# Byte positions of the weight tiles, LN1 in pairs with two evicting engines, and earlier FFN sums in a one-core decoder layer

## Chip, cores and metric

One Trainium2 chip, one core. The metric is the device time of one execution in microseconds (us). The kernel before takes 1160.0 us, the median of 3 runs (1159.33 to 1160.42).

## What is computed

One layer of a hybrid decoder on 512 tokens of width 1024, in float32:

```python
proj = x @ w_in
q, k, v, f_logit, z, xbc, dt_raw, gate_logit = split(proj)
attn_d = forgetting_attention(q, k, v, log_f) @ w_proj_attn
ssm_d = mamba2_branch(z, xbc, dt_raw, ...) @ w_proj_ssm
mixed = (gates[0] * attn_d + gates[1] * ssm_d) @ w_out
x = layer_norm(alpha * x + mixed, ln1_g, ln1_b)                  # LN1
h = (silu(x @ w_ffn_gate) * (x @ w_ffn_up)) @ w_ffn_down         # FFN, hidden width 2816
x = layer_norm(alpha * x + h, ln2_g, ln2_b)
```

## The kernel before

All large products run on TensorE in float32r with both operands split in a high and a low part (`split`, L81: ScalarE copies the high part, VectorE subtracts it). `mm3` (L115) then issues three matmuls, high x high, low x high and high x low, into one PSUM bank. Weights come through four `raw` tiles, three `whi` and three `wlo` tiles, all of 4 KB per partition (`stile`, L71).

The order of the work is the program's order on each engine, as a scheduler lays it out; the tile pools make an engine wait where a buffer is still in use. The stages are: the input projection with the attention and the Mamba-2 heads, group by group; the branch gates and `w_proj_attn`; `w_out` by two pairs of token tiles (`wo_half`, L843); LN1; the FFN; the down projection (`gemm_down`, L153, with `evac_res`, L687); the second layer norm with the output.

**LN1.** `wo_half` leaves the sums of a token tile in `xr[tt]` with the statistics of its two halves. `moments` (L692) makes mean and variance (VectorE) and the power -1/2 (POOL), and `normalise` (L846) scales the 1024 columns, one token tile after the other. `x1_transposed` (L850) turns eight 128x128 blocks on TensorE into two PSUM banks and evicts each block with an ACTIVATE (scale and bias per partition) into `xf`.

**FFN.** The gate and up products use seven half-size products in place of eight (Strassen-like), named P1 to P7, on blocks of 512 hidden columns (the sixth has 256): classes `Gemm` (L732) and `ffn_block` (L822). There are 12 Gemms, G0, U0, G1, U1 and so on (gate, up). Each uses the weight quarters a11, a12, a22 and two sums of quarters, s1 and s3. A sum is loaded by two DMAs (`load`, L750): SP's queue copies the first quarter, then POOL's queue adds the second one to it in place. `op` (L762) makes the high and low part (`wh`, `wl`) of one product's weights; for P6 and P3 VectorE first adds two loaded tiles (L766, L768). `multiply` (L788) has 24 matmuls of 256 streamed columns (12 in the last block), so the 12 Gemms have 10 x 7 x 24 + 2 x 7 x 12 = 1848. The weights are the stationary operand here; the streamed ones are `b11`, `b21`, `nt1`, `nt2`, `t3`, `b22`, `t4`, made of `xf`. The products run in this order: `rest` (L933) lists them, `op` runs two products ahead, and loads are issued here:

```python
        if p_ == "P7" and i + 3 < len(rest):
            rest[i + 3][0].load("a11", "a12", "s1")
        if p_ == "P4" and i + 1 < len(rest):
            rest[i + 1][0].load("s3", "a22")
```

The eight tiles `rq0` to `rq7` hold the loaded quarters in a ring (L756); G0 and U0 have places written out by hand (L862).

**Down projection.** The hidden tiles (`T` for block 0, then `ht...`) are stationary and the weights `whi`, `wlo` are streamed, 512 columns each: 22 x 4 x 2 x 3 = 528 matmuls.

**Byte positions.** A tile's position in a partition follows from the sizes of the tiles allocated before it. All the large tiles are multiples of 512 bytes, so what differs between stages is a position modulo 512. Call the *distance* of a matmul the start of the stationary operand less that of the streamed one, modulo 512. Before: up to `w_out` every distance of such products is 0. In the FFN `b11`, `b21` lie at 448 and the other streamed tiles at 320; the weight tiles of the pool `wop0` lie at 448 and those of `wop1` at 320. Pairs of products alternate between the pools, so half of the FFN's matmuls have distance 0 and half 128 or 384. In the down projection `whi`, `wlo` lie at 448 and the hidden tiles at 320: distance 384.

Of the kernel before, what the change touches and what calls it, by code (L numbers as in the profile page):

```python
# [17 lines left out]
P = 128  # L18
# [19 lines left out]
def tile_hybrid_decoder_layer(  # L38
# [8 lines left out]
    nc = tc.nc  # L47
    x, out = x[0], out[0]
# [17 lines left out]
    sba = pool(right1, "sba", "right")  # L66
    rawp = pool(right1, "rawp", "right")
    wst = pool(right1, "wst", "right")
    stream = {"raw": (rawp, 4), "whi": (wst, 3), "wlo": (wst, 3)}

    def stile(tag, dtype):  # L71
        p_, n = stream[tag]
        return p_.tile([P, 1024], dtype, name=tag, bufs=n)

    ident = cst0.tile([P, P], F32, name="ident")
    make_identity(nc, ident)
    neghalf = cst0.tile([P, 4], F32, name="neghalf")
# [10 lines left out]
    def cps():  # L88
        return psum.tile([P, T], F32, name="cps", bufs=4)
# [1 line left out]

    BUFS = {"v": 2, "th": 2, "bT": 2, "cT": 2, "btok": 2, "cbm": 2, "xst": 2, "xdt": 2, "hn": 2, "ab": 6, "y": 4,
            "dx": 1, "yo": 1, "xw": 1, "sq": 1, "xtok": 2, "gz": 1, "nw": 1, "uh": 1, "ul": 1, "sd": 4}
    HOME = {t: sba for t in ("hn", "ab", "y", "dx", "yo", "xw", "sq", "nw")}
    HOME["sd"] = sdp

    def slot(tag, shape=(P, T), dtype=F32):
# [346 lines left out]
    for p_ in ("uh", "ul"):  # L444
        t = big(p_, 2)
# [243 lines left out]
        nc.vector.scalar_tensor_tensor(out=o, in0=o, scalar=ALPHA, in1=ps, op0=ALU.mult, op1=ALU.add)  # L689
        nc.vector.bn_stats(out=st6[tt][:, half, :], in_=o)  # L690

    def moments(tt):  # L692
        mv = cst0.tile([P, 4], F32, name="mv", bufs=2)
        nc.vector.bn_aggr(out=mv[:, 0:2], in_=st6[tt])
        nc.vector.tensor_scalar(out=mv[:, 2:3], in0=mv[:, 1:2], scalar1=EPS, scalar2=None, op0=ALU.add)
        nc.gpsimd.tensor_tensor(out=mv[:, 2:3], in0=mv[:, 2:3], in1=neghalf[:, 0:1], op=ALU.pow)
        return mv

    def layer_norm(tt, gb, parts=1):
        mv = moments(tt)  # L700
# [31 lines left out]
    class Gemm:  # L732
# [17 lines left out]
        def load(self, *names):  # L750
            src = {"a11": ((1, 1),), "a12": ((1, 2),), "s1": ((2, 1), (2, 2)), "s3": ((2, 1), (1, 1)), "a22": ((2, 2),)}
            for nm in names:
                if self.slots:
                    i = self.slots[nm]
                else:
                    i, rq_order[0] = rq_order[0], (rq_order[0] + 1) % 8  # L756
                t = self.raw[nm] = rqp.tile([P, 1024], F32, name="rq", tag=f"rq{i}", bufs=1)[:, 0:4 * self.F]
                nc.sync.dma_start(out=self.v(t), in_=self.q(*src[nm][0]))
                for s_ in src[nm][1:]:
                    nc.gpsimd.dma_start(out=self.v(t), in_=self.q(*s_), accum_op=ALU.add)  # L760

        def op(self, p_):  # L762

            r = self.raw
            if p_ == "P6":
                nc.vector.tensor_tensor(out=r["a11"], in0=r["s1"], in1=r["a11"], op=ALU.add)  # L766
            elif p_ == "P3":
                nc.vector.tensor_tensor(out=r["a12"], in0=r["a11"], in1=r["a12"], op=ALU.add)  # L768
            t = r[{"P1": "a11", "P2": "a12", "P6": "a11", "P5": "s1", "P7": "s3", "P3": "a12", "P4": "a22"}[p_]]
            wp = wops[nops[0] // 2 % 2]  # L770
            nops[0] += 1
            o = [wp.tile([P, 1024], F32R, name="w" + i, bufs=2)[:, 0:4 * self.F] for i in "hl"]
            split(*o, t)
            self.ops[p_] = [self.v(i) for i in o]

# [70 lines left out]
    def normalise(tt):  # L846
        mv = moments(tt)
        nc.vector.tensor_scalar(out=xr[tt], in0=xr[tt], scalar1=mv[:, 0:1], scalar2=mv[:, 2:3], op0=ALU.subtract, op1=ALU.mult)

    def x1_transposed(tt):  # L850
        for i in range(2):
            ps = cps()
            for k in range(4):
                kt = 4 * i + k
                nc.tensor.transpose(out=ps[:, k * P:(k + 1) * P], in_=xr[tt][:, kt * P:(kt + 1) * P], identity=ident)
            for k in range(4):
                kt = 4 * i + k
# [29 lines left out]
    hb.tile([P, 8], F32, name="pad2")  # L887
    tp = pool(ctx, "tp", "left")
    top = pool(left2, "top", "left")
    wops.append(pool(left2, "wop1", "left"))  # L890
    tmp2 = pool(left2, "tmp2", "left")

    def t_tile(dtype=F32):
# [42 lines left out]
            rest += [(g_, p_) for p_ in ("P1", "P2", "P6", "P5", "P7", "P3", "P4")]  # L936
    AHEAD = 2
    for i, (g_, p_) in enumerate(rest):
        if p_ == "P7" and i + 3 < len(rest):
            rest[i + 3][0].load("a11", "a12", "s1")  # L940
        if p_ == "P4" and i + 1 < len(rest):
            rest[i + 1][0].load("s3", "a22")
        if i == 0:
            for k in range(1, AHEAD):
                rest[k][0].op(rest[k][1])
        if i + AHEAD < len(rest):
            rest[i + AHEAD][0].op(rest[i + AHEAD][1])
        g_.run(p_)
# [74 lines left out]
```

## Time and profile before

| | us |
|---|---|
| median of 3 runs | 1160.0 |
| the profiled execution | 1159.04 |
| its span (first to last instruction) | 1157.3 |
| TensorE matmuls busy | 1125.0 (97%) |
| TensorE weight loads busy | 946.7 (82%) |
| VectorE busy | 772.4 (67%) |
| ScalarE busy | 532.2 (46%) |
| GpSimd (POOL) busy | 135.3 (12%) |
| DMA | 134.2 MB, mean 116 GB/s |

The busy shares are of the whole span. Matmuls overlap each other in the pipeline, so a busy share of 97% doesn't say how fast they follow each other; for that the start of one is taken from the start of the next.

### The profile page before, as it was taken

What the parts mean: (1) busy time and instruction counts of PE and PEld (TensorE: products, weight loads), DVE (VectorE), ACT (ScalarE), POOL (GpSimd) and SP (SyncE); (2) the same over time, 40 slices, a digit from 0 to 9 for tenths busy, and PEclk for the clock granted to TensorE, in tenths of its full rate; (3) what the DMA queues carried; (4) which work ended last, traced back from release to release, by engine and by line L of the source; (5) the groups of instructions that cost most, each with busy time, mean ns of one, the idle gap of its engine ahead of it and who ended that gap; (6) DMA issues with size and microseconds to landing.
All of it is one profiled execution on the core that took longest, in us unless ns stands there. A gap on an engine that the chain in (4) does not pass through costs nothing.

```text
span 1157.3 us, 15804 instructions
## 1 busy us (share of the span) xinstructions
PE 1125.0 (97%) x6086; PEld 946.7 (82%) x6086; DVE 772.4 (67%) x1213; ACT 532.2 (46%) x928; POOL 135.3 (12%) x167
## 2 busy tenths in 40 slices
PE   7999999999999999999999999999999999999997
PEld 5887777778777788777777888888999999988885
DVE  3679964883886664888697434547787777667326
ACT  3376763453542432665566443207554454452210
POOL 3003130030231100211110000021101111100001
PEclk9999999999999999999999999999999999999999
DMA  8344243233231233221321255283767786465211
GB/s 247 91 131 127 74 126 93 73 119 100 84 100 55 91 91 91 57 59 53 92 56 56 80 158 163 85 224 88 189 145 195 175 196 155 93 230 176 92 55 73
DMA packets 115771, 134.20 MB, mean 116 GB/s; under 512 B 5636, under 2 KB 93936, under 8 KB 115568
## 3 DMA queue, kind: packets, MB, share of 16 engines
q1 hardware_dynamic: 99328, 112.80, 31.8%
q0 software_dynamic: 14640, 14.10, 7.6%
q10 hardware_dynamic: 1728, 6.29, 1.6%
q8 instruction: 48, 0.79, 0.3%
q14 instruction: 27, 0.22, 0.1%
HBM read 128.78 MB, written 4.26 MB: 115 GB/s over the span
## 4 chain that ended last, share of the span: by engine, by line
PE 49%; DVE 2%; ACT 1%; DMA 1%; issue 0%; DVEq 0%; ACTq 0%
PE gps L116 11%; PE gps L117 11%; PE gps L118 11%; PE cps L117 5%; PE cps L116 5%; PE cps L118 5%; PE cps L429 1%; PE cps L435 1%; DMA rq<-in_w_ffn_gate_dram 1%; ACT xf L858 0%; DVE xr L705 0%; PE cps L407 0%; PE cps L408 0%; DVE xr L704 0%; DVE st L690 0%
## 5 line engine op out<-in xcount | busy, mean ns | idle before, releaser
L83 DVE TENSOR_TENSOR wlo<-raw,whi 128x1024 fp32r<-128x1024 f32 x127 | 156.1, 1230 | 209.7 <-ACT whi L82 209.2
L82 ACT CAST whi<-raw 128x1024 fp32r<-128x1024 f32 x127 | 133.2, 1049 | 271.0 <-PE gps L118 109.9
L116 PE MATMUL gps<-xh,whi 128*128 128x512 f32 x456 | 181.3, 398 | 0.0
L117 PE MATMUL gps<-xl,whi 128*128 128x512 f32 x456 | 181.1, 397 | 0.0
L118 PE MATMUL gps<-xh,wlo 128*128 128x512 f32 x456 | 180.9, 397 | 0.0
L82 ACT CAST wh<-rq 128x1024 fp32r<-128x1024 f32 (+1 forms) x84 | 82.1, 981 | 105.8 <-PE cps L117 43.9
L83 DVE TENSOR_TENSOR wl<-rq,wh 128x1024 fp32r<-128x1024 f32 (+1 forms) x84 | 95.0, 1132 | 38.3 <-ACT wh L82 38.2
L116 PEld LDWEIGHTS gps<-xh,whi 128*128 128x128 f32 x456 | 85.9, 188 | 16.4 <-issue 0.2
L117 PEld LDWEIGHTS gps<-xl,whi 128*128 128x128 f32 x456 | 86.0, 189 | 16.2 <-issue 0.2
L118 PEld LDWEIGHTS gps<-xh,wlo 128*128 128x128 f32 x456 | 86.0, 188 | 15.5
L116 PE MATMUL gps<-whi,xh 128*128 128x512 f32 x192 | 75.9, 396 | 3.4 <-ACT xh L82 3.4
L118 PE MATMUL gps<-whi,xl 128*128 128x512 f32 x192 | 76.1, 396 | 0.0
L117 PE MATMUL gps<-wlo,xh 128*128 128x512 f32 x192 | 75.8, 395 | 0.0
L214 DVE SCALAR_TENSOR_TENSOR t_v<-gps,cw,t_v 128x511 f32<-128x511 f32 (+2 forms) x72 | 53.5, 745 | 3.9 <-ACT t_v L211 3.1
L118 PE MATMUL gps<-t_uh,wlo 128*128 128x512 f32 x128 | 51.0, 399 | 0.0
L117 PE MATMUL gps<-t_ul,whi 128*128 128x512 f32 x128 | 51.0, 398 | 0.0
L116 PE MATMUL gps<-t_uh,whi 128*128 128x512 f32 x128 | 50.5, 394 | 0.0
L116 PEld LDWEIGHTS gps<-whi,xh 128*128 128x128 f32 x192 | 36.6, 191 | 12.1 <-ACT xh L82 4.1
L760 POOL DMA_DIRECT2D rq<-in_w_ffn_gate_dram x12 | 15.5, 1294 | 256.8 <-DMA t_sd<-in_x_dram 164.0
L414 ACT ACTIVATE t_y<-t_y,sm 128x128 f32<-128x128 f32 (+1 forms) x64 | 35.7, 559 | 19.3 <-DVE sm L412 17.7
L296 ACT ACTIVATE t_ab<-t_ab,acum 128x128 f32<-128x128 f32 x128 | 41.4, 390 | 5.8 <-DMA t_ab<-ac_d 3.9
L117 PEld LDWEIGHTS gps<-wlo,xh 128*128 128x128 f32 x192 | 36.5, 190 | 8.0 <-DVE wlo L83 0.5
(565 smaller groups left out, 2780.6 us busy)
## 6 DMA issues: line engine op xcount, KB each, us to landing
raw<-in_w_in_dram SPq DMA_DIRECT2D x80, 512.0 KB, 3.7
rq<-in_w_ffn_gate_dram SPq DMA_DIRECT2D x25, 512.0 KB, 4.9
rq<-in_w_ffn_up_dram SPq DMA_DIRECT2D x25, 512.0 KB, 4.8
raw<-in_w_ffn_down_dram SPq DMA_DIRECT2D x22, 512.0 KB, 3.8
t_ab<-ac_d SPq DMA_DIRECT2D x32, 256.0 KB, 3.3
raw<-in_w_proj_ssm_dram SPq DMA_DIRECT2D x16, 512.0 KB, 3.4
rq<-in_w_ffn_gate_dram POOLq DMA_DIRECT2D x10, 512.0 KB, 7.8
rq<-in_w_ffn_up_dram POOLq DMA_DIRECT2D x10, 512.0 KB, 6.2
```

Source lines behind the costliest of these rows:

```text
L82: nc.scalar.copy(out=hi, in_=src)
L83: nc.vector.tensor_tensor(out=lo, in0=src, in1=hi.bitcast(F32), op=ALU.subtract)
L116: nc.tensor.matmul(out=o, lhsT=l[0], rhs=r[0], start=start, stop=False, skip_group_check=skip)
L117: nc.tensor.matmul(out=o, lhsT=l[0], rhs=r[1], start=False, stop=False, skip_group_check=skip)
L118: nc.tensor.matmul(out=o, lhsT=l[1], rhs=r[0], start=False, stop=stop, skip_group_check=skip)
L214: nc.vector.scalar_tensor_tensor(out=v[:, sh:], in0=ps[:, 0:T - sh], scalar=cw[:, k, blk:blk + 1], in1=v[:, sh:], op0=ALU.mult, op1=ALU.add)
L296: nc.scalar.activation(out=m[:, r, :], in_=m[:, r, :], func=AF.Relu, scale=-1.0, bias=acum[:, c, h:h + 1])
L414: nc.scalar.activation(out=pt[:, 0:n], in_=pt[:, 0:n], func=AF.Exp, scale=-1.0, bias=sm[:, 2:3], accum_out=sm[:, 0:1])
L429: nc.tensor.transpose(out=ps[:, o:o + P], in_=pr[i][:, kb * P:(kb + 1) * P], identity=ident)
L435: nc.tensor.matmul(out=po[:, kb * P:], lhsT=vt[:, kb, hh, :], rhs=pT[kb][j], start=kb == 0 and j == 0, stop=kb == NT - 1 and j == 1)
L760: nc.gpsimd.dma_start(out=self.v(t), in_=self.q(*s_), accum_op=ALU.add)
```

## The change

It has four parts.

- *Positions.* Small unused tiles (`offset`) are allocated between the tiles of the FFN and of the down projection. Every streamed FFN tile is then at 288 modulo 512, and the four pairs `wh`, `wl` at 480, 448, 0 and 384: distances 192, 160, 224 and 96. In the down projection the hidden tiles are at 288 and the three pairs `whi`, `wlo` at 288, 96 and 128: distances 0, 192 and 160. The tile `gz` moves to another pool of the same stage; distances up to `w_out` stay 0.
- *LN1 in pairs.* `moments` and `normalise` take two token tiles: one addition and one power for both.
- *Two engines evict.* In `x1_transposed` the first PSUM bank is evicted by four ACTIVATEs as before, the second by two TENSOR_TENSORs of VectorE over 4x128 columns (multiply, then add).
- *Loads.* a11, a12 and s1 of the next Gemm are loaded at P1 (for G1 at U0's P7, as before), s3 and a22 at P7 in place of P4. The ring is walked in the order 0, 1, 3, 4, 5, 6, 2, 7.

```diff
+HB_OFF, B_OFF, W_OFF, D_OFF = 512, 160, (0, 480, 224, 384, 352), (0, 320, 32, 320)
     def stile(tag, dtype):
-        p_, n = stream[tag]
-        return p_.tile([P, 1024], dtype, name=tag, bufs=n)
+        p_, n, *off = stream[tag]
+        if not off:
+            return p_.tile([P, 1024], dtype, name=tag, bufs=n)
+        i = at_.get(tag, 0)
+        at_[tag] = i + 1
+        if i < n and off[0]:
+            offset(p_, off[0][i], f"d{i}")
+        t = p_.tile([P, 1024], dtype, name=tag, tag=f"{tag}{i % n}", bufs=1)
...
+    def offset(p_, n, nm):
+        if n:
+            p_.tile([P, n // 4], F32, name="off" + nm)
-    HOME = {t: sba for t in ("hn", "ab", "y", "dx", "yo", "xw", "sq", "nw")}
+    HOME = {t: sba for t in ("hn", "ab", "y", "dx", "yo", "xw", "sq", "nw", "gz")}
-    def moments(tt):
-        mv = cst0.tile([P, 4], F32, name="mv", bufs=2)
-        nc.vector.bn_aggr(out=mv[:, 0:2], in_=st6[tt])
-        nc.vector.tensor_scalar(out=mv[:, 2:3], in0=mv[:, 1:2], scalar1=EPS, scalar2=None, op0=ALU.add)
-        nc.gpsimd.tensor_tensor(out=mv[:, 2:3], in0=mv[:, 2:3], in1=neghalf[:, 0:1], op=ALU.pow)
+    def moments(tts):
+        mv = cst0.tile([P, 2, 4], F32, name="mv", bufs=2)[:, 0:len(tts), :]
+        for i, tt in enumerate(tts):
+            nc.vector.bn_aggr(out=mv[:, i, 0:2], in_=st6[tt])
+        nc.vector.tensor_scalar(out=mv[:, :, 2], in0=mv[:, :, 1], scalar1=EPS, scalar2=None, op0=ALU.add)
+        nc.gpsimd.tensor_tensor(out=mv[:, :, 2], in0=mv[:, :, 2], in1=neghalf[:, 0:len(tts)], op=ALU.pow)
...
-                    i, rq_order[0] = rq_order[0], (rq_order[0] + 1) % 8
+                    i, rq_order[0] = (0, 1, 3, 4, 5, 6, 2, 7)[rq_order[0]], (rq_order[0] + 1) % 8
...
-            wp = wops[nops[0] // 2 % 2]
+            i = nops[0] % 4
+            wp, off = wpools[i]
+            if nops[0] < 4:
+                offset(wp, off, f"w{i}")
...
-            for k in range(4):
-                kt = 4 * i + k
-                nc.scalar.activation(out=xf[i][:, k, tt * P:(tt + 1) * P], in_=ps[:, k * P:(k + 1) * P], func=AF.Identity,
-                                     scale=lnv[:, kt:kt + 1], bias=lnv[:, 8 + kt:9 + kt])
+            if i == 0:
+                for k in range(4):
+                    nc.scalar.activation(out=xf[i][:, k, ts], in_=ps[:, k, :], func=AF.Identity, scale=lnv[:, k:k + 1],
+                                         bias=lnv[:, 8 + k:9 + k])
+            else:
+                g_, b_ = (lnv[:, c:c + 4].rearrange("p (k o) -> p k o", o=1).broadcast_to([P, 4, P]) for c in (4, 12))
+                nc.vector.tensor_tensor(out=xf[i][:, :, ts], in0=ps, in1=g_, op=ALU.mult)
+                nc.vector.tensor_tensor(out=xf[i][:, :, ts], in0=xf[i][:, :, ts], in1=b_, op=ALU.add)
...
+        if (p_ == "P1" or i == 0) and i + 7 < len(rest):
+            rest[i + (7 if i else 3)][0].load("a11", "a12", "s1")
         if p_ == "P7" and i + 3 < len(rest):
-            rest[i + 3][0].load("a11", "a12", "s1")
-        if p_ == "P4" and i + 1 < len(rest):
-            rest[i + 1][0].load("s3", "a22")
+            rest[i + 3][0].load("s3", "a22")
...
-    stream.update({"raw": (wst3, 4), "whi": (wst3, 3), "wlo": (wst3, 3)})
+    stream.update({"raw": (wst3, 4), "whi": (wst3, 3, D_OFF), "wlo": (wst3, 3, (0, 0, 0))})
```

On SP's queue the loads of G1 and U1 stand behind those of G0 and U0. Before, with buffer numbers: `rq_7180`, `rq_7252`, `rq_7182`, `rq_7255`, `rq_7184` are a11, s3, a12, a22 and s1 of G1; `rq_7413`, `rq_7415`, `rq_7417` are a11, a12 and s1 of U1.

```order
L758 DMA rq_7180<-in_w_ffn_gate_dram 128x4x256
L758 DMA rq_7413<-in_w_ffn_up_dram 128x4x256
L758 DMA rq_7252<-in_w_ffn_gate_dram 128x4x256
L758 DMA rq_7182<-in_w_ffn_gate_dram 128x4x256
L758 DMA rq_7255<-in_w_ffn_gate_dram 128x4x256
L758 DMA rq_7184<-in_w_ffn_gate_dram 128x4x256
L758 DMA rq_7415<-in_w_ffn_up_dram 128x4x256
L758 DMA rq_7417<-in_w_ffn_up_dram 128x4x256
```

With the change, at the same place: `rq_7171`, `rq_7175`, `rq_7173`, `rq_7178`, `rq_7181` are a11, s1, a12, s3 and a22 of G1, and `rq_7277`, `rq_7279`, `rq_7281` are a11, a12 and s1 of U1.

```order
L782 DMA rq_7171<-in_w_ffn_gate_dram 128x4x256
L782 DMA rq_7175<-in_w_ffn_gate_dram 128x4x256
L782 DMA rq_7173<-in_w_ffn_gate_dram 128x4x256
L782 DMA rq_7178<-in_w_ffn_gate_dram 128x4x256
L782 DMA rq_7279<-in_w_ffn_up_dram 128x4x256
L782 DMA rq_7181<-in_w_ffn_gate_dram 128x4x256
L782 DMA rq_7277<-in_w_ffn_up_dram 128x4x256
L782 DMA rq_7281<-in_w_ffn_up_dram 128x4x256
```

The sum s1 of G1 moves from the sixth place to the second, and its tile is `rq3` in place of `rq2`: the place that s3 of G1 had before. POOL's additions follow in the same order, s1 of G1 first.

On VectorE, between the statistics of the last token tiles and `nt1l`, the low part of the first streamed operand that needs all of `xf`, there stands before:

```order
L695 TENSOR_SCALAR mv<-mv 128x1
L83 TENSOR_TENSOR wl<-rq,wh 128x1024
L848 TENSOR_SCALAR t_sd<-t_sd,mv 128x1024
L694 BN_AGGR mv<-st_6418 128x2
L83 TENSOR_TENSOR wl<-rq,wh 128x1024
L695 TENSOR_SCALAR mv<-mv 128x1
L83 TENSOR_TENSOR wl<-rq,wh 128x1024
L848 TENSOR_SCALAR t_sd<-t_sd,mv 128x1024
L781 TENSOR_TENSOR cp<-gps,cp 128x512
L83 TENSOR_TENSOR wl<-rq,wh 128x1024
L766 TENSOR_TENSOR rq<-rq 128x1024
L768 TENSOR_TENSOR rq<-rq 128x1024
```

and behind these `T<-xf`, `T<-T,xf`, the gate's product `g`, a second `cp` and then `nt1l`. With the change, up to `nt1l`:

```order
L878 TENSOR_SCALAR t_sd<-t_sd,mv 128x1024 x2
L810 TENSOR_TENSOR cp<-gps,cp 128x512
L893 TENSOR_TENSOR xf<-cps,lnv 128x4x128
L102 TENSOR_TENSOR wl<-rq,wh 128x1024
L894 TENSOR_TENSOR xf<-xf,lnv 128x4x128
L893 TENSOR_TENSOR xf<-cps,lnv 128x4x128
L860 SCALAR_TENSOR_TENSOR g<-g,cp 128x512
L894 TENSOR_TENSOR xf<-xf,lnv 128x4x128
L944 TENSOR_TENSOR T<-xf 128x1024
L102 TENSOR_TENSOR wl<-rq,wh 128x1024
L947 SCALAR_TENSOR_TENSOR T<-T,xf 128x1024
L102 TENSOR_TENSOR nt1l<-T,nt1h 128x1024
```

Four evictions of 512 columns have come in ahead of `nt1l`; one addition of 1024 columns (that of L768) and one of 512 (the second `cp`) now stand behind it. TensorE's own order of matmuls is the same as before.

## Rows read from the trace of the kernel before

**Rows 1.** The page's part 4, shares of the chain that ended last, by engine.
```profile
PE 49%; DVE 2%; ACT 1%; DMA 1%; issue 0%; DVEq 0%; ACTq 0%
```
**Rows 2.** Waits of TensorE from 750 us on: waiter, releaser, us in total, times, longest.
```profile
PE cps L116 <- DVE cp L781: 3.6, 1, 3.6
PE gps L117 <- DVE nt1l L83: 1.8, 1, 1.8
PE cps L855 <- DVE t_sd L848: 1.0, 1, 1.0
```
**Rows 3.** Timeline of TensorE from 837 to 842 us: start, us, engine, line, what, count, idle before.
```profile
837.19 0.28 PE L118 MATMUL cps<-b22h,wl 128*128 128x256 f32 x1
841.06 0.36 PE L116 MATMUL cps<-t4h,wh 128*128 128x256 f32 x1 [3.60 <-DVE cp L781]
...
842.00 0.41 PE L116 MATMUL cps<-t4h,wh 128*128 128x256 f32 x1
842.21 0.41 PE L117 MATMUL cps<-t4l,wh 128*128 128x256 f32 x1
```
**Rows 4.** Timeline of VectorE, the same stretch.
```profile
839.09 1.23 DVE L766 TENSOR_TENSOR rq<-rq 128x1024 f32<-128x1024 f32 x1 [4.48 <-DMA rq<-in_w_ffn_gate_dram]
840.23 0.68 DVE L781 TENSOR_TENSOR cp<-cps,cp 128x512 f32<-128x512 f32 x1
```
**Rows 5.** Timeline of SP's queue: the copies of s3 and s1 of G1.
```profile
816.93 0.37 SPq L758 DMA_DIRECT2D rq<-in_w_ffn_gate_dram  x1
...
826.04 0.37 SPq L758 DMA_DIRECT2D rq<-in_w_ffn_gate_dram  x1
```
**Rows 6.** Timeline of POOL: the additions for s3 and s1 of G1.
```profile
822.22 1.29 POOL L760 DMA_DIRECT2D rq<-in_w_ffn_gate_dram  x1 [16.10 <-DMA rq<-in_w_ffn_gate_dram]
831.98 1.27 POOL L760 DMA_DIRECT2D rq<-in_w_ffn_gate_dram  x1 [8.47 <-DVE g L831]
```
**Rows 7.** The page's part 6: count, KB each, us from issue to landing.
```profile
rq<-in_w_ffn_gate_dram POOLq DMA_DIRECT2D x10, 512.0 KB, 7.8
```
**Rows 8.** Three stretches: length, busy us (count) by engine, PEclk, DMA share, GB/s.
```profile
860.00:1020.00 160.00, 160.00 (x1344) 160.00 (x1343) 120.34 (x142) 79.78 (x105) 20.56 (x16) 1.00 0.68 159
...
810.90:814.30 3.40, 3.40 (x19) 3.40 (x18) 3.40 (x4) 0.80 (x1) 0.00 (x0) 0.50 0.05 10
841.60:845.00 3.40, 3.40 (x19) 3.40 (x18) 3.38 (x5) 0.00 (x0) 0.00 (x0) 0.50 0.01 2
```
**Rows 9.** Timeline of VectorE around 805 us.
```profile
801.10 0.68 DVE L781 TENSOR_TENSOR cp<-gps,cp 128x512 f32<-128x512 f32 x1
...
808.90 1.22 DVE L83 TENSOR_TENSOR nt1l<-T,nt1h 128x1024 fp32r<-128x1024 f32 x1
```
**Rows 10.** Chain of waits, 730 to 830 us: start, us, what.
```profile
780.95 1.75 PE cps L855 x16
...
800.31 5.60 ACT xf L858 x16
```
**Rows 11.** Timeline of TensorE: the start that `nt1l` held up.
```profile
810.17 0.39 PE L117 MATMUL gps<-nt1l,wh 128*128 128x256 f32 x1 [1.75 <-DVE nt1l L83]
```
**Rows 12.** Timeline of TensorE: starts at both ends of four runs.
```profile
655.21 0.39 PE L117 MATMUL gps<-xl,whi 128*128 128x512 f32 x1
...
677.19 0.39 PE L118 MATMUL gps<-xh,wlo 128*128 128x512 f32 x1
...
873.94 0.28 PE L118 MATMUL cps<-nt2h,wl 128*128 128x256 f32 x1
...
879.63 0.28 PE L118 MATMUL cps<-t3h,wl 128*128 128x256 f32 x1
...
885.27 0.28 PE L117 MATMUL cps<-t4l,wh 128*128 128x256 f32 x1
...
1058.98 0.40 PE L117 MATMUL cps<-wlo,ht21h 128*128 128x512 f32 x1
...
1072.70 0.39 PE L116 MATMUL cps<-whi,ht40h 128*128 128x512 f32 x1
```

More of the change, by code (lines that the diff above doesn't have):

```diff
@@ L69, in tile_hybrid_decoder_layer @@
     stream = {"raw": (rawp, 4), "whi": (wst, 3), "wlo": (wst, 3)}
+    at_ = {}
     def stile(tag, dtype):
-        p_, n = stream[tag]
-        return p_.tile([P, 1024], dtype, name=tag, bufs=n)
+        p_, n, *off = stream[tag]
[6 more added lines that the diff above has]
+        t = p_.tile([P, 1024], dtype, name=tag, tag=f"{tag}{i % n}", bufs=1)
+        if i == n - 1 and tag == "wlo":
+            offset(p_, D_OFF[3], "de")
+        return t
+    def offset(p_, n, nm):
+        if n:
+            p_.tile([P, n // 4], F32, name="off" + nm)
     ident = cst0.tile([P, P], F32, name="ident")
@@ L690, in evac_res @@
         nc.vector.bn_stats(out=st6[tt][:, half, :], in_=o)
-    def moments(tt):
-        mv = cst0.tile([P, 4], F32, name="mv", bufs=2)
-        nc.vector.bn_aggr(out=mv[:, 0:2], in_=st6[tt])
-        nc.vector.tensor_scalar(out=mv[:, 2:3], in0=mv[:, 1:2], scalar1=EPS, scalar2=None, op0=ALU.add)
-        nc.gpsimd.tensor_tensor(out=mv[:, 2:3], in0=mv[:, 2:3], in1=neghalf[:, 0:1], op=ALU.pow)
+    def moments(tts):
[4 more added lines that the diff above has]
+        nc.gpsimd.tensor_tensor(out=mv[:, :, 2], in0=mv[:, :, 2], in1=neghalf[:, 0:len(tts)], op=ALU.pow)
         return mv
     def layer_norm(tt, gb, parts=1):
-        mv = moments(tt)
+        mv = moments([tt])[:, 0, :]
         for i in range(parts):
@@ L714, in tile_hybrid_decoder_layer @@
     rqp = pool(right2, "rqp", "right")
-    wops = [pool(right2, "wop0", "right")]
+    wop = pool(right2, "wop0", "right")
     nops = [0]
+    wpools = [(wop, W_OFF[0]), (wop, W_OFF[1])]
     def h_tile(b):
@@ L769, in op @@
             t = r[{"P1": "a11", "P2": "a12", "P6": "a11", "P5": "s1", "P7": "s3", "P3": "a12", "P4": "a22"}[p_]]
-            wp = wops[nops[0] // 2 % 2]
+            i = nops[0] % 4
+            wp, off = wpools[i]
+            if nops[0] < 4:
+                offset(wp, off, f"w{i}")
             nops[0] += 1
-            o = [wp.tile([P, 1024], F32R, name="w" + i, bufs=2)[:, 0:4 * self.F] for i in "hl"]
+            o = [wp.tile([P, 1024], F32R, name="w" + x, tag=f"w{x}{i}", bufs=1)[:, 0:4 * self.F] for x in "hl"]
+            if nops[0] == 2:
+                offset(wp, W_OFF[4], "we")
             split(*o, t)
@@ L844, in wo_half, with normalise @@
         gemm_down(wo_chunk, KD, tok(mx), (2 * th_, 2 * th_ + 1), half, evac_res, gps)
-    def normalise(tt):
-        mv = moments(tt)
-        nc.vector.tensor_scalar(out=xr[tt], in0=xr[tt], scalar1=mv[:, 0:1], scalar2=mv[:, 2:3], op0=ALU.subtract, op1=ALU.mult)
+    def normalise(tts):
+        mv = moments(tts)
+        for i, tt in enumerate(tts):
+            nc.vector.tensor_scalar(out=xr[tt], in0=xr[tt], scalar1=mv[:, i, 0:1], scalar2=mv[:, i, 2:3], op0=ALU.subtract, op1=ALU.mult)
     def x1_transposed(tt):
+        ts = slice(tt * P, (tt + 1) * P)
         for i in range(2):
-            ps = cps()
+            ps = cps().rearrange("p (k t) -> p k t", k=4)
             for k in range(4):
                 kt = 4 * i + k
-                nc.tensor.transpose(out=ps[:, k * P:(k + 1) * P], in_=xr[tt][:, kt * P:(kt + 1) * P], identity=ident)
-            for k in range(4):
-                kt = 4 * i + k
-                nc.scalar.activation(out=xf[i][:, k, tt * P:(tt + 1) * P], in_=ps[:, k * P:(k + 1) * P], func=AF.Identity,
-                                     scale=lnv[:, kt:kt + 1], bias=lnv[:, 8 + kt:9 + kt])
+                nc.tensor.transpose(out=ps[:, k, :], in_=xr[tt][:, kt * P:(kt + 1) * P], identity=ident)
+            if i == 0:
[6 more added lines that the diff above has]
+                nc.vector.tensor_tensor(out=xf[i][:, :, ts], in0=xf[i][:, :, ts], in1=b_, op=ALU.add)
         nc.gpsimd.dma_start(out=x1_d[tt], in_=xr[tt])
@@ L866, in tile_hybrid_decoder_layer @@
     wo_half(0, 0)
-    for tt in (0, 1):
-        normalise(tt)
+    normalise((0, 1))
     G0.op("P1")
@@ L877, in tile_hybrid_decoder_layer @@
         split(*xop[nm], B[k, 1])
+    offset(bop, B_OFF, "b")
     wo_half(1, 1)
-    for tt in (2, 3):
-        normalise(tt)
+    normalise((2, 3))
     G0.multiply("P1")
@@ L886, in tile_hybrid_decoder_layer @@
     hb = pool(ctx, "hb", "left")
-    hb.tile([P, 8], F32, name="pad2")
+    offset(hb, HB_OFF, "hb")
     tp = pool(ctx, "tp", "left")
     top = pool(left2, "top", "left")
-    wops.append(pool(left2, "wop1", "left"))
+    wop = pool(left2, "wop1", "left")
+    wpools += [(wop, W_OFF[2]), (wop, W_OFF[3])]
     tmp2 = pool(left2, "tmp2", "left")
```

## The prediction

> **What bounds the kernel now.** Read the chain of waits first: TensorE holds 49% of the span on it and no other engine over 2% [rows 1]. So a change pays where TensorE waits, or where its matmuls follow each other faster. The list of waits from 750 us on has three places where TensorE waits [rows 2]: 3.6 us for the addition `cp` (L781), 1.8 us for `nt1l`, 1.0 us for the second normalised tile. The timelines tell why. At 837.19 a matmul starts, the next at 841.06 [rows 3]: 3.87 us where about 0.12 is usual. VectorE had stood idle for 4.48 us before its L766 addition of a11 and s1 of G1, until a DMA landed, and the `cp` that TensorE needed stood behind it [rows 4]. The sum s1 was late because SP issued its copy at 826.04 [rows 5] and POOL its addition at 831.98 [rows 6].
>
> Behind this gap, and behind that before `nt1l`, the granted clock falls from 1.00 to 0.50, the lower of the two levels (1.2 GHz), for 3.4 us each [rows 8]. In there 256-column matmuls start 0.21 us apart [rows 3].
>
> The other thing to read is the step, start to start, inside runs without waits [rows 12]. 512 columns: 97 steps from 655.21 to 677.19 are 226.6 ns each at distance 0; 59 steps from 1058.98 to 1072.70, in the down projection at distance 384, are 232.5. 256 columns: 48 steps from 873.94 to 879.63 at distance 128 are 118.5 ns; 47 steps from there to 885.27 at distance 0 are 120.0. Half the FFN is of either kind, 119.25 on the average. TensorE never waits in the 160 us from 860 to 1020 [rows 8], so these differences are not waits for another engine.
>
> **Loads.** s1 of G1 takes the place of s3 in the ring and nearly in SP's queue: `rq3` came free for a copy at 816.93, which POOL's addition followed at 822.22 [rows 5, 6]. An addition lands 7.8 us after its issue in the median [rows 7], so s1 should be there near 830. VectorE came to its L766 at 839.09 less 4.48, thus 834.6 [rows 4]: about 4.6 us to spare. The wait goes, and with it 3.87 - 0.12 = 3.75 us. The slow stretch behind it goes too: 3.4 us at 0.213 are 16 matmuls, each 0.094 slower than 0.119: 1.5 us. What is late next? s3 of G1 is copied two or three places later than before, but is used only by P7, two products (5.7 us) behind P6; later Gemms had no wait of TensorE and load earlier now. POOL's additions keep their number, and SP's queue only changes order, so no cost there.
>
> **LN1.** The first pair of token tiles is hidden: TensorE goes straight from `wo_half` to the transposes. For the second pair the chain ends in `nt1l`, which started at 808.90 and released TensorE at 810.17 [rows 9, 11]. VectorE had hardly a pause before it, so its sum of work decides, not ScalarE's sixteen ACTIVATEs of 5.60 us [rows 10], half of which go. Ahead of `nt1l` VectorE gains four evictions of 512 columns, bounded by the 0.68 of the like `cp` [rows 9]: up to +2.7. It loses one 1024-column addition (1.23 [rows 4]) and one `cp` (0.68), which move behind, and one of two short waits for POOL's power. That leaves 0.3 or less. I take 0, with -1.0 to +1.5 as bounds (overlap of starts on one side; a late PSUM bank, for which the evictions wait in VectorE's order, on the other). TensorE ends its products of `b11`, `b21` a little sooner and waits longer for `nt1l`, so what faster steps save before 810 is lost there, and the slow stretch at 810.9 stays.
>
> **Positions, FFN.** 1848 matmuls less the 96 of the first two products of G0 and U0, which end ahead of the `nt1l` wait: 1752. New distances 192, 160, 224, 96: none of them stands in the trace. Bounds: 16 transposes of 128 columns take 1.75 us [rows 10], 109.4 ns each, the shortest spacing of full weight loads; and 125.9, if the new distances add to the 120.0 what 384 adds to 226.6 at 512 columns (5.9). The same shape at the tried distances, 118.5 and 120.0, is the nearest row. I take 117.0, as far below the better one as the worse one is above it: (119.25 - 117.0) x 1752 = 3.9 us. VectorE is at 75% and DMA at 0.68 there [rows 8], so both can follow a step 2% shorter.
>
> The Trainium skill (TensorE: Matmul & The Clock Gate, Back-to-back issue gap) gives N/2.4 + 2.5 ns for an isolated gap, 109.2 for 256 and 215.8 for 512 columns; estimated by it, the FFN would give 17.6 us and the down projection 8.8 at the most. No run of matmuls of these two shapes above is that short.
>
> **Positions, down projection.** 528 matmuls at 232.5. A third of them gets distance 0, 226.6 by [rows 12]; for 160 and 192 I take half way, 229.5, between 226.6 and 232.5 as ends. The mean is 228.5: 4.0 x 528 = 2.1 us (1.0 to 3.1).
>
> **Sum.** 3.75 + 1.5 + 0 + 3.9 + 2.1 = 11.2 us off the profiled execution's 1159.04, which lies 1.0 under the median of the runs. Off the median, 1160.0: 1148.8.
>
> **Rivals.**
> 1. *The positions do nothing* (chance 0.20): only the loads pay, 1160.0 - 5.25 = 1154.8. For it: the four-way mean is already within 1.5 ns of either kind. Against: two steps for one shape in waitless runs [rows 12]. A rule of the Trainium skill speaks for it (same page, Step-by-step: what each phase is for): PE has two independent SBUF read ports, and loading the next weights takes no bandwidth from the running matmul. By that rule 1154.8 is the time; [rows 12] lean against it, though stages with different distances differ in other things too.
> 2. *The new distances clear whatever lengthens the step* (0.12): 109.4 in the FFN, 9.85 x 1752 = 17.3, and 226.6 in all of the down projection, 3.1: 1160.0 - 5.25 - 20.4 = 1134.3. For it: transposes run that close. Against: no product here does.
> 3. *The sum is still late* (0.08), behind another copy in SP's or POOL's order: only the 6.0 of the positions remain, 1154.0. Against: the 4.6 us to spare.
> 4. *Slower* (0.06): the new distances lengthen the FFN's step to the 125.9 above, 6.65 x 1752 = 11.7 us, against 5.25 saved: 1166.4. It decides from 119.25 + 5.25/1752 us, 122.25 ns, on. For it: at 512 columns one distance costs 5.9 ns. Against: at 256 columns the distance off 0 was the better one.
>
> **How the numbers follow.** The forecast has 0.47; 0.07 is left for smaller mishaps, such as a longer LN1 chain. The range leaves out rival 2's lower end and rival 4: 1137 to 1157; the forecast's own is 1142 to 1154. A measurement of this kernel can tell some 0.2%, 2.3 us, from no change. Faster by more: the forecast, rivals 1 to 3 and nothing else, 0.87. Within: the mishaps, 0.07. Slower: rival 4, 0.06.
>
> **What would show it.** In the profile after, TensorE's wait for `cp` near 837 and the slow stretch behind it are gone, and SP's copy for s1 stands near 817; the wait for `nt1l` and the stretch of 0.50 behind it remain; the steps in waitless runs are near 117 ns and 228 ns; the span up to 790 us is as before. I am wrong if the steps don't move, if they grow, or if VectorE still waits for a DMA at its first L766 of `rest`.

## The result and the profile after

| | before | after |
|---|---|---|
| median, us | 1159.66 (4 runs, 1159.03 to 1160.42) | 1152.16 (4 runs, 1150.45 to 1153.12) |
| ratio, with its 95% interval | | 0.9933 [0.9916, 0.9951] |
| the profiled execution, us | 1159.04 | 1153.12 |
| its span, us | 1157.3 | 1151.4 |

The change saves 7.5 us by the medians; the prediction said 1148.8, a gain of 11.2. The two profiled executions lie only 5.9 apart: the one after was the slowest of its four. Where those 5.9 us come from is read off by following one matmul through both traces. TensorE runs the same 6086 matmuls in the same order, so the n-th start of one trace can be set beside the n-th of the other (us from the span's start):

| up to | before | after | gained in this part |
|---|---|---|---|
| the start of the last quarter of `w_out` | 782.46 | 784.36 | -1.9 |
| the first matmul that needs `nt1l` | 810.17 | 812.09 | 0.0 |
| the last matmul ahead of the late sum | 837.19 | 837.38 | 1.7 |
| 79 matmuls behind it | 851.91 | 846.73 | 5.4 |
| the last matmul of the FFN | 1025.63 | 1019.07 | 1.4 |
| the fifth start behind it | 1026.92 | 1021.53 | -1.2 |
| the last matmul | 1148.45 | 1142.12 | 0.9 |
| the end | 1157.33 | 1151.41 | -0.4 |

The chain's shares by engine, after (compare [rows 1]):

```profile
PE 44%; DVE 3%; issue 3%; DMA 2%; ACT 1%; POOL 0%; DVEq 0%; POOLq 0%; ACTq 0%; SPq 0%
```

TensorE's waits from 750 us on, after (waiter, releaser, us in total, times, longest), against [rows 2]:

```profile
PE gps L136 <- DVE nt1l L102: 1.1, 1, 1.1
PE cps L886 <- DVE t_sd L878: 0.8, 1, 0.8
PE gps L135 <- ACT nt1h L101: 0.6, 1, 0.6
PE cps L135 <- ACT whi L101: 0.6, 1, 0.6
PE cps L136 <- DVE wlo L102: 0.3, 1, 0.3
```

The 3.6 us for `cp` are gone; the last two rows are new, and so is the one for `nt1h`. The timelines of SP's queue, of POOL and of VectorE show why the wait for `cp` is gone:

```profile
815.57 0.37 SPq L782 DMA_DIRECT2D rq<-in_w_ffn_gate_dram  x1
818.94 0.37 SPq L782 DMA_DIRECT2D rq<-in_w_ffn_gate_dram  x1
...
823.47 1.30 POOL L784 DMA_DIRECT2D rq<-in_w_ffn_gate_dram  x1 [11.45 <-DVE T L963]
...
834.77 1.22 DVE L790 TENSOR_TENSOR rq<-rq 128x1024 f32<-128x1024 f32 x1
835.91 0.68 DVE L810 TENSOR_TENSOR cp<-cps,cp 128x512 f32<-128x512 f32 x1
```

The copy at 815.57 is G1's a11, the one at 818.94 its s1 (826.04 before, [rows 5]); POOL adds at 823.47 (831.98, [rows 6]), which lands at 830.82; and VectorE's first L790 of `rest` starts at 834.77 with no idle time ahead of it, where [rows 4] had 4.48 us.

Two stretches after, as in [rows 8]: the FFN, and a place near 62.8 us where the granted clock is low now and was not before. There is no stretch at 0.50 near 811 or 841 us any more. (Both traces have one near 15 us and one behind the last matmul.)

```profile
860.00:1015.00 155.00, 155.00 (x1313) 155.00 (x1312) 116.24 (x137) 77.71 (x104) 19.96 (x16) 1.00 0.68 157
62.80:66.20 3.40, 3.40 (x12) 2.36 (x11) 1.93 (x6) 1.88 (x5) 0.00 (x0) 0.50 0.00 0
```

TensorE's timeline gives the steps. Each pair of neighbouring rows below is 24 steps of one distance: in the FFN 224, 96, 192 and 160, in the down projection 0, 192 and 160.

```profile
828.90 0.28 PE L137 MATMUL gps<-b22h,wl 128*128 128x256 f32 x1
...
831.70 0.28 PE L137 MATMUL gps<-t4h,wl 128*128 128x256 f32 x1
...
834.55 0.28 PE L137 MATMUL cps<-t3h,wl 128*128 128x256 f32 x1
...
837.38 0.28 PE L137 MATMUL cps<-b22h,wl 128*128 128x256 f32 x1
...
840.25 0.28 PE L137 MATMUL cps<-t4h,wl 128*128 128x256 f32 x1
...
1037.21 0.39 PE L135 MATMUL cps<-whi,ht11h 128*128 128x512 f32 x1
...
1042.68 0.40 PE L135 MATMUL cps<-whi,ht20h 128*128 128x512 f32 x1
...
1048.19 0.39 PE L135 MATMUL cps<-whi,ht21h 128*128 128x512 f32 x1
...
1053.79 0.39 PE L135 MATMUL cps<-whi,ht30h 128*128 128x512 f32 x1
```

That is 2.80/24 = 116.7 ns, then 118.7, 117.8 and 119.9 (from starts to the nanosecond, which the rows round to 10): 118.3 on the average (119.25 before). In the down projection it is 227.9, 229.6 and 233.6: 230.4 (232.5 before). Over the whole down projection, with its last pieces that follow another order, it is 230.6 after and 232.4 before.

Ahead of the down projection TensorE meets its new waits, and SP's first copy of `w_ffn_down` is late: 15.1 us ahead of the FFN's last matmul before, 4.1 now. SP's queue before, then SP's queue and TensorE after:

```profile
1010.57 18.96 SPq L106 DMA_DIRECT2D raw<-in_w_ffn_down_dram  x7
```

```profile
1015.00 14.03 SPq L125 DMA_DIRECT2D raw<-in_w_ffn_down_dram  x8
...
1019.93 0.96 PE L135 MATMUL cps<-whi,T 128*128 128x512 f32 x3 [0.59 <-ACT whi L101]
1021.19 0.50 PE L136 MATMUL cps<-wlo,T 128*128 128x512 f32 x1 [0.30 <-DVE wlo L102]
```

### The profile page after: what moved, and what is told of

Same layout as the page of the kernel before. It is cut to its first block, busy times and chain, and to the rows that moved or that the text cites. A ratio compares the mean times of both kernels' runs of the same rounds, so it can differ in the third digit from the quotient of the medians.

```text
span 1151.4 us, 15793 instructions
## 1 busy us (share of the span) xinstructions
PE 1121.1 (97%) x6086; PEld 942.4 (82%) x6086; DVE 776.6 (67%) x1219; ACT 528.4 (46%) x912; POOL 133.8 (12%) x165
## 4 chain that ended last, share of the span: by engine, by line
PE 44%; DVE 3%; issue 3%; DMA 2%; ACT 1%; POOL 0%; DVEq 0%; POOLq 0%; ACTq 0%; SPq 0%
PE gps L135 9%; PE gps L136 9%; PE gps L137 9%; PE cps L136 5%; PE cps L137 5%; PE cps L135 5%; DMA rq<-in_w_ffn_up_dram 1%; PE cps L448 1%; PE cps L454 1%; DMA t_sd<-in_x_dram 0%; DVE xr L726 0%; PE cps L426 0%; DMA raw<-in_w_ffn_down_dram 0%; PE cps L427 0%; DVE wlo L102 0%
```

## The experiments

Each kernel of the decoder was timed against the kernel before on the same chip (medians of 1158.8 to 1159.6 there). Single executions scatter: 17 of the kernel before lie between 1156.63 and 1160.93.

**Parts of the change taken back, one at a time.** Old positions:

```diff
-HB_OFF, B_OFF, W_OFF, D_OFF = 512, 160, (0, 480, 224, 384, 352), (0, 320, 32, 320)
+HB_OFF, B_OFF, W_OFF, D_OFF = 32, 0, (0, 0, 0, 0, 0), (0, 0, 0, 0)
```

> The changed kernel with the distances of before (0, 128 and 384). By the prediction's terms (3.9 + 2.1 us) it is 6.0 us slower than the changed kernel: 1158.2. By the steps read from the trace after (FFN 118.3, down projection 230.7) the positions are worth 1.7 + 0.95 us, less a new wait of 0.9 us ahead of the down projection: 1.7 us slower, 1153.9. If the positions do nothing (rival 1): 1152.2 or less.

Measured: 1153.17 (five runs, 1151.69 to 1154.24; ratio to before 0.9952 [0.994, 0.9965]), 1.0 over the changed kernel. Its trace has 119.2 ns in the FFN and 232.4 in the down projection, as before, and no wait for `whi`. So the positions are worth little of the 7.5: 1.0 us by the medians, 2.2 by the ratios, whose intervals overlap, and 1.6 by the steps of the two traces (1.7 + 0.9, less 1.0 at the start of the down projection), not the 6.0 of the prediction. SP's first copy of `w_ffn_down` stands 5.2 us ahead of the FFN's last matmul here:

```profile
1015.40 14.26 SPq L125 DMA_DIRECT2D raw<-in_w_ffn_down_dram  x8
```

So the new order of the loads alone delays this copy by 9.8 of the 11.0 us, but at 5.2 us TensorE doesn't wait yet. With the changed positions the copy stands at 4.1, with the old loads (below) as with the new, and TensorE waits.

Old LN1:

```diff
-    normalise((2, 3))
+    for tt in (2, 3):
+        normalise((tt,))
...
-            if i == 0:
+            if True:
                 for k in range(4):
```

(the same for tiles 0 and 1, and with `lnv` columns that follow `i`).

> The changed kernel with LN1 token tile by token tile, all evictions by ScalarE. By the prediction (0, with -1.0 to +1.5): between 1150.7 and 1153.2, nt1l releases TensorE at the same place. By the trace after, in which the slow stretch behind nt1l is gone: the wait before nt1l grows from about 1.1 to 1.8 us or more, the granted clock falls to 0.50 for 3.4 us behind it, and the time is 2 to 2.5 us longer: 1154.4. Rival: the stretch went because of the positions; then it stays away here, and returns in the kernel with the old positions.

Measured: 1151.49 (five runs, 1151.09 to 1152.49; ratio 0.994 [0.9927, 0.9953]). LN1 is worth nothing: from the start of the last quarter of `w_out` to the start that `nt1l` holds up it takes 27.74 us here, 27.73 in the changed kernel and 27.71 before. The slow stretch did not come back either, in spite of a step of 2.06 us at `nt1l`. The kernel with the old positions, whose LN1 is the new one, has it at 811.7. So neither the LN1 code nor the length of the wait decides it. In the profiled executions of all versions, those below too, a stretch of 3.4 us at 0.50 stands near 62 us (five of them, the changed kernel, old LN1 and old loads among these), near 811 us (four, before and old positions among these) or at neither place (two), and in none at both; the kernel with 64 and 0 below has none in one execution and one at 62.7 us in another. So it can come and go without an edit.

Old loads:

```diff
-        if (p_ == "P1" or i == 0) and i + 7 < len(rest):
-            rest[i + (7 if i else 3)][0].load("a11", "a12", "s1")
-        if p_ == "P7" and i + 3 < len(rest):
-            rest[i + 3][0].load("s3", "a22")
+        if p_ == "P7" and i + 3 < len(rest):
+            rest[i + 3][0].load("a11", "a12", "s1")
+        if p_ == "P4" and i + 1 < len(rest):
+            rest[i + 1][0].load("s3", "a22")
```

(with the ring in the order 0 to 7).

> The changed kernel with the load calls and the ring order of before. By the prediction the wait for cp near 837 us returns (3.75 us) with a slow stretch of 1.5 us behind it: 1157.4. If only the wait comes back: 1155.9. If something else in the change hid the late sum: 1152.2.

Measured: 1159.26 (twelve runs, 1158.13 to 1162.73; ratio 1.0005 [0.9995, 1.0015]): the whole gain is gone. It is more than the 5.25 us of the prediction, since the sum is later here than before. VectorE's timeline (against [rows 4]) and the stretch at 0.50, which begins inside TensorE's wait of 6.8 us (TensorE is busy for 3.08 us of it):

```profile
842.25 1.22 DVE L790 TENSOR_TENSOR rq<-rq 128x1024 f32<-128x1024 f32 x1 [7.62 <-DMA rq<-in_w_ffn_gate_dram]
...
840.50:847.30 6.80, 3.08 (x14) 3.11 (x15) 5.05 (x6) 1.05 (x1) 1.04 (x1) 0.50 0.56 80
```

From the matmul ahead of the gap to the 79th behind it 17.73 us pass, 14.72 before and 9.35 in the changed kernel. So in the changed kernel the loads are worth 8.4 us at this place. Why POOL's addition, issued at 832.80, took longer to land than the one before, no run shows.

**The step by itself.** A kernel without the decoder: 96 matmuls for each distance, the stationary tile sliced at another column each time.

```diff
+        s = [t[:, (d + base) // 4 % 128:] for t in st]
+        m = [t[:, base // 4:] for t in mv]
...
+                for a, b in ((0, 0), (0, 1), (1, 0)):
+                    nc.tensor.matmul(out=ps[:, 0:n], lhsT=s[a][:, sk], rhs=m[b][:, mk], start=i == 0, stop=i == nm - 1)
```

> No decoder layer: only runs of 96 matmuls of float32r without any wait, in groups of three as in the kernel, at each distance 0, 32, ... 480, for 512 and 256 streamed columns, once alone and once with VectorE additions and DMA loads beside them; 256 columns at two positions of the streamed tile. Theory A (the distance alone sets the step): the steps of the kernel's trace come back whether other work runs beside or not; 256 columns: 0 at 119.9, 96 at 118.7, 128 at 118.6, 160 at 119.9, 192 at 117.8, 224 at 116.7, 384 at 118.6 ns; 512 columns: 0 at 226.7, 160 at 233.8, 192 at 229.8, 384 at 232.4 ns. Theory B (other engines' accesses set it, the distances of a stage only go with them): alone, all distances agree within 0.5 ns per shape; with other work beside them, all steps are longer alike. Theory C (the place of the streamed tile matters, not the distance): the two positions of the streamed tile differ by 1 ns or more at equal distances.

Measured, ns per step, each over 80 to 82 steps from start to start:

| distance modulo 256 | 0 | 32 | 64 | 96 | 128 | 160 | 192 | 224 |
|---|---|---|---|---|---|---|---|---|
| 256 columns | 120.0 | 118.4 | 113.3 | 120.0 | 118.6 | 120.0 | 113.3 | 116.7 |
| 512 columns | 226.7 | 233.3 | 233.3 | 234.2 | 232.4 | 233.3 | 228.9 | 233.3 |

A distance and the same plus 256 agree within 0.2 ns. So do both positions of the streamed tile, and the runs with and without VectorE's additions and DMA beside them. Theories B and C fall; A holds, with 256 as the modulus, but for two entries: 192 is at 117.8 in the changed kernel and 96 at 118.7.

A rule of the Trainium skill that spoke for rival 1 (TensorE: Matmul & The Clock Gate, Step-by-step: what each phase is for) says that loading the next weights takes no read bandwidth from the running matmul. The table doesn't fit it: with nothing else running, the position of the weights alone moves the step by 6.7 ns at 256 and 7.5 at 512 columns. The measurement decides on the time; whether read bandwidth is what the weights take, or why the distance matters at all, no run shows.

**Why 192 has two values.** The same, with the FFN's own loop and mixtures of distances, 24 matmuls to each:

```diff
+        for j in range(2):
+            for k in range(4):
+                sk = slice(k * 256 + j * P, k * 256 + (j + 1) * P)
```

> No decoder layer: runs of matmuls without a wait, but now with the loop of the FFN (24 matmuls to a pair of weight tiles, two halves of four) and the streamed tile at 288 as there. It is to tell why 256 columns at distance 192 took 113.3 ns alone but 117.8 in the changed kernel (96: 120.0 and 118.7). Theory H (what ran before decides: a pair starts in the rhythm that the pair before it left): the cycle 192, 160, 224, 96 gives about 117.8, 119.9, 116.7 and 118.7, and 192 all the time 113.3. Theory P (the place of the streamed tile decides): at 288 also the pure 192 gives 117.8, and the cycle at 160 gives 113.3. Theory K (something else in the kernel lengthens it): 113.3 at 192 everywhere here, 120.0 at 96. At 512 columns the cycle 0, 192, 160 gives 228.4, 229.8 and 233.8 by H, and 226.7 at 0 in any case where it stands alone or with 256.

Measured: the cycle 192, 160, 224, 96 gives 117.8, 119.9, 116.7 and 118.7 with the streamed tile at 160, and within 0.2 of these at 288: the kernel's numbers, so K and P fall. But 192 all the time gives 117.8 too, and mixed with 64 it gives 113.3. H's number for 192 alone fails as well; what stays of it is that 192 has two rhythms, 113.3 and 117.8, and what ran before chooses. 64 was 113.3 in every mixture. The distance isn't all for 96 either: 120.0 in the first loop, 118.7 all the time in this one, 117.2 beside 192. At 512 columns 0 and 256 are 226.7, and the changed kernel's cycle of 0, 192 and 160 gives 228.4, 228.9 and 233.6.

**Other positions in the whole kernel.** The FFN all at 192, with the down projection at 0 or as changed:

```diff
+HB_OFF, B_OFF, W_OFF, D_OFF = 512, 160, (0, 0, 192, 0, 320), (0, 0, 0, 160)
...
+HB_OFF, B_OFF, W_OFF, D_OFF = 512, 160, (0, 0, 192, 0, 320), (0, 320, 32, 320)
```

> The changed kernel with all four weight pairs of the FFN at distance 192 and all tiles of the down projection at distance 0. By the steps of the runs without a wait (113.3 and 226.7): (118.3 - 113.3) x 1752 + (230.7 - 226.7) x 528 = 8.8 + 2.1 us, and the new wait ahead of the down projection goes (0.9), since its raw tiles lie again on single rq tiles: 1140.4. If 192 stays at the 117.8 of the changed kernel: 0.9 + 2.1 + 0.9 us, 1148.3. If positions do nothing: 1152.2.

> The changed kernel with all four weight pairs of the FFN at distance 192, the down projection as changed. By the runs without a wait: 8.8 us less, 1143.4, and the wait ahead of the down projection stays. With 117.8: 1151.3. If positions do nothing: 1152.2.

Measured: 1147.52 (four runs, 1146.53 to 1148.14; ratio 0.99 [0.9884, 0.9915]) and 1150.3 (five runs, 1149.6 to 1151.6; 0.9924 [0.9912, 0.9937]). Both lie about 1 us under the expectation with 117.8, and the traces show that step throughout. With 0 in the down projection the step there is 226.7 and TensorE's wait for `whi` is gone; SP's first copy of `w_ffn_down` is issued 5.2 us ahead of the FFN's last matmul, as with the old positions, not 4.1. In the changed kernel the `raw` tiles lie across two `rq` tiles each; with all offsets of the down projection at 0 they lie on single ones.

The FFN at 64 and the down projection at 0:

```diff
+HB_OFF, B_OFF, W_OFF, D_OFF = 512, 160, (0, 0, 64, 0, 448), (0, 0, 0, 160)
```

> The kernel with all pairs of the FFN at 192 and all tiles of the down projection at 0 (1147.5), its four pairs moved to 64. If the steps of the runs without a wait carry over (64: 113.33 alone and in every mixture): (117.78 - 113.33) x 1752 = 7.8 us less, 1139.7, as long as the loads and VectorE follow. If the FFN has another floor of 117.8, set by VectorE or the loads: 1147.5. If a wait for a sum comes back with the shorter products: between the two, with the wait named in the chain.

Measured: one execution at 1139.71, the profiled one, and four at 1146.41 to 1146.89; median 1146.47, ratio 0.9874 [0.9854, 0.9893]. Its fastest execution is the fastest here; its median can't be told from the 1147.09 of the positions alone, below. In TensorE's timeline the starts near 830 us and at the end of the FFN, for this kernel and then for the one with 192 and 0:

```profile
830.03 0.28 PE L136 MATMUL cps<-t3l,wh 128*128 128x256 f32 x1
...
1008.30 0.28 PE L137 MATMUL cps<-t4h,wl 128*128 128x256 f32 x1
```

```profile
830.01 0.28 PE L137 MATMUL cps<-t3h,wl 128*128 128x256 f32 x1
...
1016.22 0.28 PE L137 MATMUL cps<-t4h,wl 128*128 128x256 f32 x1
```

1573 steps in 178.27 us are 113.3 ns, 1581 in 186.21 are 117.8. VectorE and the loads keep up with the shorter one. For the four slower executions there is no trace, so the kernel ran once more:

> The kernel with 64 and 0 once more, for its trace: one execution took 1139.7 with steps of 113.33 in the FFN, four took 1146.4 to 1146.9 without a trace. If 64 has two rhythms, as 192 has (113.3 and 117.8 in the runs without a wait), an execution near 1146.5 shows 117.8 in the FFN, no longer wait and the same 226.7 in the down projection; (117.78 - 113.33) x 1752 = 7.8 us would then be the difference. If a wait (a sum, the loads) makes it: the steps are 113.3 again and the chain names some 7 us of waits. An execution near 1139.7 repeats the first trace and settles nothing.

Measured: 1140.54, again with 113.3. It repeats the first and settles nothing. The last kernel asks the step by itself again, 72 matmuls at 64, 192 or 224 after 32 entries each; a ScalarE copy of `gap` columns into the stationary tile makes the wait:

```diff
+        if gap:
+            nc.scalar.copy(out=st[0][:, 0:gap], in_=raw[0][:, 0:gap])
```

> No decoder layer: runs of 72 matmuls of 256 columns at distance 64, 192 or 224, each entered in 32 ways: from 24 matmuls at each of the sixteen distances, and after sixteen waits of TensorE for ScalarE of different length. If 64 and 192 have each two rhythms and the entry picks one: both 113.3 and 117.8 appear at 64 as at 192, and runs stay in the one they began with; then the 6.8 us between executions of the kernel with 64 can be the rhythm. If only 192 has two: 64 is 113.3 after every entry, and that difference has another cause. 224: 116.7 after every entry, or 117.8 as it had next to 192.

Measured: 64 has both rhythms. After runs at the sixteen distances it is 113.3 seven times and 117.8 nine times; after the sixteen waits, which grow by some 54 ns each (the second by 109), the two alternate. 192 is 113.3 after 0, 64, 256 and 320 and 117.8 after every other distance and every wait. In the first loop it had been 113.3 behind 160, so the distance ahead alone doesn't choose. 224 is 116.7 after every wait and fourteen distances, 117.8 after 128 and 384. TensorE's timeline for two neighbouring waits at 64, both ends of 60 steps each:

```profile
574.12 0.38 PE L75 MATMUL ps<-mvh,sth 128*128 128x256 f32 x1 [0.50 <-ACT sth L80]
...
575.04 0.28 PE L75 MATMUL ps<-mvl,sth 128*128 128x256 f32 x1
...
582.11 0.28 PE L75 MATMUL ps<-mvl,sth 128*128 128x256 f32 x1
...
583.53 0.39 PE L75 MATMUL ps<-mvh,sth 128*128 128x256 f32 x1 [0.55 <-ACT sth L80]
...
584.33 0.28 PE L75 MATMUL ps<-mvh,sth 128*128 128x256 f32 x1
...
591.13 0.28 PE L75 MATMUL ps<-mvh,sth 128*128 128x256 f32 x1
```

7.07/60 = 117.8 ns after a wait of 0.50 us, 6.80/60 = 113.3 after 0.55. A rhythm, once entered, stays to the end of the run. So the 6.8 us between executions of the kernel with 64 fit the second rhythm over 1752 matmuls (7.8 us, if it held in all of them). The granted clock doesn't make them: its mean is 0.996 in the fast execution and 0.996 to 0.998 in the four. That the rhythm did in those four is argued, not shown; a wait isn't excluded.

**Positions alone, and the far end.** The kernel before with 64 and 0 and nothing else; and the changed kernel with the FFN at 0 and the down projection at 160:

```diff
+HB_OFF, B_OFF, W_OFF, D_OFF = 512, 160, (0, 0, 0, 0, 512), (352, 0, 0, 320)
```

> The kernel before with these positions alone (64 in the FFN, 0 in the down projection); LN1 and loads as before. By the steps: (119.25 - 113.33) x 1752 + (232.5 - 226.7) x 528 = 10.4 + 3.1 us less than before, 1145.4. If the late sum of G1 is fixed by DMA and not by TensorE, the wait for cp grows by what the products ahead of it save (some 0.2 ms of it lie ahead, 192 matmuls, 1.1 us): 1146.5. If positions do nothing: 1158.9.

> The changed kernel with all of the FFN at distance 0 and all of the down projection at 160, nothing else moved. By the steps (120.0 and 233.6): (120.0 - 118.3) x 1752 + (233.6 - 230.7) x 528 = 3.0 + 1.5 us more than the changed kernel, 1156.7. If positions do nothing: 1152.2. It is the other end to the kernel with 64 and 0, whose work and order are the same: by the steps the two differ by 11.7 + 3.6 = 15.3 us, and by some waits.

Measured: positions alone 1147.09 (six runs, 1145.67 to 1152.63; ratio 0.9895 [0.9876, 0.9913]). The steps are 113.3 and 226.7, and the late sum costs more than before, as the second theory has it (the products that it puts ahead of the sum, 192 matmuls, take 23 us, not 0.2 ms):

```profile
PE cps L135 <- DVE cp L810: 5.3, 1, 5.3
...
839.40:846.20 6.80, 3.56 (x17) 3.59 (x18) 5.54 (x7) 1.05 (x1) 0.00 (x0) 0.50 0.46 71
```

(TensorE's wait, and the stretch at 0.50, now 6.8 us long, of which TensorE is busy for 3.56: it begins inside the wait.) The far end took 1156.81 (seven runs, 1154.55 to 1158.33; ratio 0.9972 [0.9961, 0.9983]) with steps of 120.0 and 233.3, where 1156.7 was expected; that the two agree to 0.1 us is luck, at such a scatter. So the same work in the same order takes from 1146.5 to 1156.8 by the medians, by the bytes at which the tiles begin, and 1139.7 in the fastest execution.

## Why the prediction was right, and where its sizes were off

The time, 1152.16, lies within the range of 1137 to 1157 and on the side forecast. But the range holds rivals 1 and 3 as well, and the time lies nearer to rival 1 (1154.8) than to the forecast (1148.8): it is the traces that tell them apart. By the prediction's own steps:

- **Loads: right.** Gap and slow stretch, 5.25 us expected, gave 5.4 in the traces (837 to 852 us). s1 was copied at 818.94 (near 817 said) and VectorE came to it at 834.77 (834.6 said) without a wait; POOL's addition had landed at 830.82 (830 said). The versions show that this carries most of the gain: the one with the loads and the old positions saves 5.9 us by the medians (1153.17 against 1159.11 there), the one without the loads nothing (1159.26).
- **LN1: right in size, 0.** The evictions moved to VectorE fit into what pairing saved and what moved behind `nt1l`: from VectorE's first addition for the second pair to the start of `nt1l` 16.6 us pass before and after, and TensorE's part takes 27.73 us against 27.71. The wait for `nt1l` remains, as said (1.1 us, and 0.6 for `nt1h` ahead of it). That the slow stretch stays behind it was wrong for this execution, and the reason given, the wait, doesn't decide it: with old positions it follows the same waits, with old LN1 it doesn't follow a longer one. In the accounts this is nothing: 1.5 us gained there, 1.6 lost at 62.8. Another 0.3 is lost elsewhere up to 782 us, where the prediction had the span unchanged.
- **Positions, FFN: that they matter was right, the size was off.** The term that failed is the 117.0, set as far below the better tried distance as the worse one lay above it. The four new distances measure 117.8, 119.9, 116.7 and 118.7, together 118.3: (119.25 - 118.3) x 1752 = 1.7 us in place of 3.9. The bounds, 109.4 and 125.9, held. No row gave the sign: two of the four, 119.9 and 118.7, are longer than the better distance of before (118.5), so that the mean came out shorter was in part luck.
- **Positions, down projection: the same.** The failed term is half way for 160 and 192, 229.5: 192 is there (229.6), 160 is the longer, at 233.6 above even 384, outside the ends I had set. Distance 0 among the others is 227.9: the first six of its 24 steps behind another distance are 229 to 236 ns, the rest 226.7. Over the whole 230.6 for 228.5, against 232.4 before: 0.9 us in place of 2.1.
- **Left out: the start of the down projection.** The offsets also shift the `raw` tiles, which then share memory with two `rq` tiles each. The first copy of `w_ffn_down` is issued 4.1 us ahead of the FFN's last matmul, in place of 5.2 with the new loads alone, and TensorE waits 0.9 us: 1.2 lost against the kernel before, 1.0 against the old positions, and with it all that the down projection's new steps gain. The prediction has no term for this.

The terms as measured, 5.4 + 0 + 1.7 + 0.9, less 1.2 for the new wait, 0.3 up to 782 us and 0.4 behind the last matmul, make 6.1; 5.9 lie between the two spans and 7.5 between the medians, and single executions scatter by more than these differ.

The rivals. That positions do nothing (1154.8) falls by the steps and by the versions with medians from 1146.5 to 1156.8, though for this choice of positions it was within 3 us of the truth. That they clear everything (1134.3) falls too: no distance reaches 109.4 at 256 columns, though 0 had 226.7 at 512. 64 in its shorter rhythm gives (119.25 - 113.3) x 1752 = 10.4 of that rival's 17.3 us. By the Trainium skill (TensorE: Matmul & The Clock Gate, Back-to-back issue gap) the isolated gaps are estimated at 109.2 and 215.8; the shortest runs here, 113.3 and 226.7, stay 4.1 and 10.9 above them. The sum still late, and the longer FFN step: neither came.

## What to carry to other kernels

Measure the step, start to start, in runs without a wait for each pair of tile positions before choosing any: here one run of a bare loop gave the whole table, and it speaks for one distance (64 at 256 columns, 0 at 512) where the change mixes four. Enter each distance in several ways, since that loop showed only one of the two rhythms of 64. And check the choice in the kernel's own trace: the table gave 113.3 for 192, the kernel 117.8. A move of bytes or a new order of buffers moves what the first loads of the next stage wait for, so look at these as well. And two gains that meet at one wait don't add: shorter products made the late sum cost 5.3 us of waiting in place of 3.6, and with the loads in time the same positions cost nothing there.

## What the runs showed of the hardware that was not expected

- The step of float32r matmuls with a weight load each depends on the start of the weights less that of the streamed tile, modulo 256 bytes, from 113.3 to 120.0 ns at 256 columns and from 226.7 to 234.2 at 512 (bare loop). The best distance for one shape is not that for the other (64: 113.3 and 233.3).
- At 64 and 192 there are two steady rhythms, 113.3 and 117.8, entered by what ran before; 96 had 120.0 in one loop and 118.7 in another. Waits that differ by some 54 ns alternate between them at 64.
- A stretch of 3.4 us at 0.50 appears behind LN1's waits in some executions and near 62 us, right behind matmuls of 16 columns, in others. At the longer waits for the late sum (6.8 and 5.3 us) it was 6.8 us long and began inside the wait; behind the one of 3.6 us it was 3.4.
